# Low weight parts by accumulating DMAs in the first five pairs, no arithmetic on GpSimd in the turn, and a later T3, in a two-layer encoder kernel

## The chip, the cores and the metric

The kernel runs on one core of a Trainium2 chip. A core has five engines, each with its own in-order queue: TensorE (PE in the profile, with PEld for its weight loads), VectorE (DVE), ScalarE (ACT), GpSimd (POOL) and SyncE (SP), which here only issues DMAs. The metric is the device time of one execution in microseconds (us).

## The reference, cut to what matters

Two layers of a streaming encoder over 16 + 1024 frames of width 1024. Each layer has an attention part and then a gated feed-forward part; the change lies at the seam between the two.

```python
h = h + jnp.concatenate([o_gla, o_fox], axis=-1) @ w_out[i]
h = h + conv_ffn(rms_norm(h, ffn_norm[i]), w_up[i], conv_w[i], conv_b[i], w_down[i])

def conv_ffn(x, w_up, conv_w, conv_b, w_down):
    h = x @ w_up
    ...
    u, g = jnp.split(hc, 2, axis=-1)
    return (jax.nn.silu(g) * u) @ w_down
```

`w_up` is 1024 by 2 x 2816; between the product and the gate stands a causal depthwise convolution of width 3. Everything is float32. The kernel keeps that precision on PE by splitting each operand into a high part, rounded to the type fp32r, and a low part, the rest; one product is three matrix products (high x high, low x high, high x low).

## The kernel before

**Layout.** Activations are held transposed: 128 channels on the partitions, frames along the free axis. The frames are cut into two halves of 520 (516 in the last layer, which drops the meta frames at the end).

**Output projection** (`wout`, L1083). Eight tiles of output channels, first over one half of the frames, then over the other. After each tile DVE adds the result to the residual (L1095), POOL stores it to memory (L1096), ACT squares it and the square is added to an accumulator `acc` (L1102): on POOL, except for the last two tiles of the second half, on DVE. `scale(h)` turns `acc` of a half into the normalising factor: a matmul with ones, then DVE, ACT twice, DVE three times (L1074, L271 to L275). In the second half the operands of the first half of the frames are already made (`first_operand`, L1079) between the tiles.

**Up projection** (`ffn_up`). The 22 pairs of a `u` and a `g` tile are multiplied by a scheme of Strassen and Winograd: the blocks are (first or second half of the inner dimension) by (first or second half of the frames) and each pair takes seven products instead of eight. The products are numbered p = 1 to 7. Each has a weight operand (`up_operand`) and an activation operand `X[p]`:

| p | weight operand | activation operand | made by |
|---|---|---|---|
| 1, 2 | A11, A12 | the scaled first half | `first_operand` |
| 6 | S2 = S1 - A11 | T2 | `make_t23` |
| 7 | A11 - A21 | T3 | `make_t23` |
| 4 | A22 | N4 | `make_n4` |
| 5 | S1 = A21 + A22 | T1 | `make_t1` |
| 3 | A12 - S2 | B22 | `make_b22` |

The activation operands are made once per layer, in the turn from the output projection to the up projection. `put` makes the two parts of each: a cast on ACT (L1037), a subtraction on DVE (L1038). T2 takes a multiplication (L1132) and an addition (L1133) on DVE ahead of that for each of its four tiles; N4 a subtraction on POOL (L1144); T1 an operation on DVE (L1151) and a subtraction on POOL (L1152).

**Order.** PE's order is written out in `seq`: (0,1), (0,2), (1,1), (1,2), (2,1), (2,2), then (0,6), (1,6), (0,7), (1,7), (0,4), (1,4), (0,5), (1,5), (0,3), (1,3), then the rest of pair 2, then pair after pair, (pair, product) each. A product is 24 matmuls: four tiles of the inner dimension, two chunks of frames, three parts. `before` says ahead of which position each activation operand is written into the program: 1 `second_half` (the factor of the second half), 2 `make_t23`, 7 `make_n4`, 9 `make_t1`, 12 `make_b22`. The order on the other engines is made ahead of time by a scheduler, which takes the instruction earliest in the program among those that it takes to be ready; once made it is fixed, and each engine waits at the head of its queue.

**Banks.** Products gather in eight PSUM banks, two per accumulator. The second product of pairs 0, 1 and 2 uses the same two banks for all three pairs (`place`): (1,2) can start when (0,2) has been added out, and (2,2) when (1,2) has, by the DVE addition L1180. Products 1, 6, 7 and 4 are copied out by ACT (L1181).

**Weights.** SP loads quarter blocks of 256 KB into buffers. A11 and A12 have four buffers of their own (`raw`); A21, A22, S1, S2 and the two blocks of pair 2 that are needed early share seven (`raw2`). DVE makes the combinations (L997). `up_split` makes the parts, in six buffers each (three for even, three for odd positions): the high one with a cast on ACT (L1013), the low one with a subtraction on DVE (L1014). `ensure(i)` prepares operands up to four positions ahead of the product.

After product 3 of a pair come the convolution (ACT L1169, DVE L1173), the gate (L1198, L1202) and the store of the result by a DMA that POOL issues (L1203).

Of the kernel before, what the change touches and what calls it, by code (L numbers as in the profile page):

```python
# [10 lines left out]
F32 = mybir.dt.float32  # L11
# [3 lines left out]
ALU = mybir.AluOpType  # L15
# [33 lines left out]
HALVES, HALVES_LAST = (0, 520, 520), (8, 524, 516)  # L49
AHEAD = 4  # L50
NSPLIT = 4


class Slots:
# [78 lines left out]
class Kern:  # L133
# [731 lines left out]
    def attention(self, lyr, nm, hsrc, chunks, feed):  # L865
        tc, nc, s = self.tc, self.nc, self.slots
        with tc.tile_pool(name=f"aps{lyr}", bufs=2, space=PSUM, reuse_waits="tile") as pp2, \
# [50 lines left out]
            with tc.tile_pool(name=f"att{lyr}", bufs=2, reuse_waits="tile") as ap, \  # L918
# [5 lines left out]
                def plan(p):  # L924
# [11 lines left out]
                    elif p == 4:  # L936
# [10 lines left out]
                        def split(j):  # L947
                            c0, n = CH[j]
                            for k in KORD:
                                self.split(mix[k][0][:, c0:c0 + n], mix[k][1][:, c0:c0 + n], land[k][:, c0:c0 + n])  # L950
                            for m in range(NSPLIT):
                                nc.gpsimd.dma_start(hT[m][:, c0:c0 + n], hsrc[m][:, c0:c0 + n])
                        split(2)
                        for m in range(NSPLIT):
                            def ev(ps, c0, n, m=m):
                                h = hT[m][:, c0:c0 + n]
                                nc.vector.tensor_tensor(out=h, in0=ps, in1=h, op=ALU.add)
# [3 lines left out]
                self.fox(lyr, ap, pp, qs, plan, lambda: box["mix"][KD - 1])  # L961
            for m in range(NSPLIT, KD):
                nc.sync.dma_start(box["hT"][m][:, chunks[0][0]:T], hsrc[m][:, chunks[0][0]:T])
# [15 lines left out]
    def up_operand(self, lyr, j, p, fw, raws, odd):  # L979
        nc = self.nc  # L980
        if j == 2 and p in (1, 2):
            src = fw.tile([128, 4, 128], F32, tag="raw2", name="raw2")
            nc.sync.dma_start(src[:], self.wm[lyr, M_UP + 4][:, 4 * p - 4:4 * p, :])
            return self.up_split(src, fw, odd)
        if j not in raws:
            u, g = self.wm[lyr, M_UP + 2 * j], self.wm[lyr, M_UP + 2 * j + 1]
            q = raws[j] = {}
            for name, src, k0, own in (("A11", u, 0, True), ("A21", g, 0, False), ("A22", g, 4, False), ("A12", u, 4, True)):
                q[name] = self.wp.tile([128, 4, 128], F32, tag="raw", name="raw", bufs=4) if own else \
                    fw.tile([128, 4, 128], F32, tag="raw2", name="raw2")  # L990
                nc.sync.dma_start(q[name][:], src[:, k0:k0 + 4, :])
        q = raws[j]

        def combine(out, a, b, op):
            if out not in q:
                q[out] = fw.tile([128, 4, 128], F32, tag="raw2", name="raw2")
            nc.vector.tensor_tensor(out=q[out][:], in0=q[a][:], in1=q[b][:], op=op)  # L997
        if p == 6:
            combine("S1", "A21", "A22", ALU.add)
            combine("S2", "S1", "A11", ALU.subtract)  # L1000
        elif p == 7:
            combine("A21", "A11", "A21", ALU.subtract)
        elif p == 3:
            combine("A12", "A12", "S2", ALU.subtract)
        src = q[{1: "A11", 2: "A12", 3: "A12", 4: "A22", 5: "S1", 6: "S2", 7: "A21"}[p]]
        return self.up_split(src, fw, odd)

    def up_split(self, src, fw, odd):
        nc = self.nc
        pool, x = (fw, "2") if odd else (self.wp, "")  # L1010
        hi = pool.tile([128, 4, 128], F32R, tag="hi" + x, name="hi", bufs=3)
        lo = pool.tile([128, 4, 128], F32R, tag="lo" + x, name="lo", bufs=3)
        nc.scalar.copy(hi[:], src[:])  # L1013
        nc.vector.tensor_tensor(out=lo[:], in0=src[:], in1=hi[:].bitcast(F32), op=ALU.subtract)  # L1014
        return [(hi[:, k, :], lo[:, k, :]) for k in range(4)]

    def ffn_up(self, lyr, mix, hT, pp, fw, halves, o0, during_last):
        nc, s = self.nc, self.slots
        W = halves[2]
        n = W // 2  # L1020
        sl = [slice(c, c + W) for c in halves[:2]]
# [10 lines left out]
        def operand(x):  # L1032
            X[x] = [[s.get(F32R, f"x{x}", (128, 2, 520)) for _ in range(2)] for _ in range(2)]

        def put(x, k, src, lo=None):
            hi_, lo_ = (X[x][i][k // 2].t[:, k % 2, :W] for i in range(2))
            nc.scalar.copy(hi_, src)  # L1037
            (lo or nc.vector).tensor_tensor(out=lo_, in0=src, in1=hi_.bitcast(F32), op=ALU.subtract)  # L1038
# [17 lines left out]
        def ensure(i):  # L1056
            while len(ops) < min(i + AHEAD + 1, len(seq)):
                ops.append(self.up_operand(lyr, *seq[len(ops)], fw, raws, len(ops) % 2))


        acc, sq = s.get(F32, "r"), half_slot("sq")
# [5 lines left out]
        def scale(h):  # L1067

            ps, r = bank2("ssq", 3), acc[:, sl[h]]
            for c in range(2):  # L1070
                nc.tensor.matmul(ps[:, c, :n], self.ones[:], acc[:, halves[h] + c * n:halves[h] + c * n + n],
                                 start=True, stop=True)
            vv, y0, a = half(tmp[0], 0), half(tmp[0], 1), half(tmp[1], 0)
            nc.vector.tensor_scalar(out=two(vv), in0=used(ps), scalar1=1.0 / D, scalar2=EPS, op0=ALU.mult, op1=ALU.add)  # L1074
            self.rsqrt(r, vv, y0, a)
# [7 lines left out]
        def wout(i, h):  # L1083
            m = orders[h][i]
            k0 = KD - 1 if m < NSPLIT else 0

            def f(w):
                if h == 1 and i == KD - 1:
                    ensure(0)
                ps = bank2("wo", i % 4)  # L1090
                for k in range(len(w)):
                    for c in range(2):
                        self.mm3(ps[:, c, :n], w[k], mix[k0 + k], halves[h] + c * n, n, k == 0, k == len(w) - 1)
                x = hT[m][:, sl[h]]
                nc.vector.tensor_tensor(out=two(x), in0=used(ps), in1=two(x), op=ALU.add)  # L1095
                nc.gpsimd.dma_start(self.hm[m][:, sl[h]], x)  # L1096
                if i == 0:
                    nc.scalar.activation(acc[:, sl[h]], x, AF.Square)
                else:
                    t = half(sq, i % 2)  # L1100
                    nc.scalar.activation(t, x, AF.Square)
                    (nc.vector if h and i > 5 else nc.gpsimd).tensor_tensor(out=acc[:, sl[h]], in0=acc[:, sl[h]], in1=t, op=ALU.add)  # L1102
                if h == 0:
                    return
                if m < NSPLIT:
                    nc.scalar.mul(half(gt, m % 2), x, gain(m))
                else:
                    nc.vector.scalar_tensor_tensor(out=diff(m - 4), in0=x, scalar=gain(m), in1=half(gt, m % 2),
                                                   op0=ALU.mult, op1=ALU.subtract)
                if i == 1:  # L1110
                    scale(0)
                    operand(1)
                    operand(2)
                for k in turn.get(i, ()):
                    first_operand(k)
            return (self.wm[lyr, M_WO + m][:, k0:KD, :], f)
# [5 lines left out]
        lowk, highk, t0, t1 = hT[:4], hT[4:], sl[0], sl[1]  # L1122
# [2 lines left out]
            scale(1)  # L1125
            s.put(sq, *tmp)

        def make_t23():
            operand(6)
            for k in range(4):  # L1130
                x, y = diff(k), lowk[k][:, t0]
                nc.vector.tensor_tensor(out=x, in0=x, in1=acc[:, t1], op=ALU.mult)  # L1132
                nc.vector.tensor_tensor(out=y, in0=x, in1=y, op=ALU.add)  # L1133
                put(6, k, y)
            operand(7)
            for k in range(4):
                put(7, k, diff(k))
            s.put(*dd)

        def make_n4():  # L1140
            operand(4)
            for k in range(4):
                x = highk[k][:, t0]
                nc.gpsimd.tensor_tensor(out=x, in0=x, in1=lowk[k][:, t0], op=ALU.subtract)  # L1144
                put(4, k, x)

        def make_t1():
            operand(5)
            for k in range(4):
                x, y = highk[k][:, t1], lowk[k][:, t0]  # L1150
                nc.vector.scalar_tensor_tensor(out=x, in0=x, scalar=gain(4 + k), in1=acc[:, t1], op0=ALU.mult, op1=ALU.mult)  # L1151
                nc.gpsimd.tensor_tensor(out=y, in0=x, in1=y, op=ALU.subtract)  # L1152
                put(5, k, y)
            s.put(acc, *lowk)

        def make_b22():
            operand(3)
            for k in range(4):
                put(3, k, highk[k][:, t1])
            s.put(*highk)  # L1160
        before = {1: second_half, 2: make_t23, 7: make_n4, 9: make_t1, 12: make_b22}


        st = {}
# [45 lines left out]
        for i, (j, p) in enumerate(seq):  # L1210
# [3 lines left out]
            q = st.setdefault(j, {})  # L1214
# [219 lines left out]
```

## Time and profile before

| | |
|---|---|
| median of 3 runs | 2649.35 us (2644.81 to 2653.99) |
| profiled execution | 2645.09 us, of which the span from first to last instruction is 2643.3 |
| mean granted PE clock | 0.987 |
| busy in the span | PE 95%, PEld 91%, DVE 67%, ACT 47%, POOL 17% |
| DMA | 240.72 MB, mean 91 GB/s |
| turn of layer 0, turn of layer 1 | around 590 to 670 us, around 1898 to 1980 us |

Busy rows give the time in which an engine worked; a PE row does not tell that PE was at full clock, which the granted clock in the windows does. In rows of groups the first number behind the bar is the time in all, the second the mean in ns of one, and behind the second bar stands the idle time of the engine just before, with what ended it. In rows by source line three numbers are the shortest, the median and the longest in ns. Instructions of one engine that follow each other closely overlap a little: a DVE instruction listed with 0.69 us starts 0.61 us after the one before.

### The profile page before, as it was taken

Reading aid. Unit: us, or ns where it says so; the run is one execution under the profiler, and the core shown is the slowest. Engines: PE = TensorE matmul, PEld = TensorE weight load, DVE = VectorE, ACT = ScalarE, POOL = GpSimd, SP = SyncE. Lnnn points to the kernel's source line nnn. Section 1 sums busy time; section 2 is a strip of 40 time slices with the busy share of each in tenths; the row PEclk is TensorE's granted clock in tenths of the full one; section 3 lists DMA queues with packets and bytes.
Section 4 is the critical chain, followed back from the end, with each engine's and each line's share of the span. In section 5 each row is a group of like instructions: output and inputs, shape, how many; then the busy total and the mean of one; then the engine's idle time right before and its main releaser. Section 6 shows DMA issues by size and latency. Waiting matters only on the chain.

```text
span 2643.3 us, 46336 instructions
## 1 busy us (share of the span) xinstructions
PE 2523.9 (95%) x18102; PEld 2407.2 (91%) x18102; DVE 1759.9 (67%) x3484; ACT 1240.1 (47%) x2677; POOL 457.9 (17%) x596
## 2 busy tenths in 40 slices
PE   8999999897999999999999999998989999999997
PEld 7988898897999999999999888887889999998886
DVE  7655676759877777643665666666698767776335
ACT  6345665645544445421343565665455444453112
POOL 4033333333000000000201333332320000000002
PEclk9999999998999999999999999999999999999999
DMA  3222124341222222632312222142512222245222
GB/s 125 65 83 70 47 83 124 106 131 58 97 81 76 85 77 92 217 94 58 103 56 65 75 72 74 56 138 91 158 51 85 83 81 77 83 139 189 65 55 77
DMA packets 114476, 240.72 MB, mean 91 GB/s; under 512 B 14432, under 2 KB 36192, under 8 KB 114256
## 3 DMA queue, kind: packets, MB, share of 16 engines
q1 hardware_dynamic: 96000, 182.27, 22.7%
q0 software_dynamic: 16384, 53.18, 5.5%
q8 instruction: 142, 2.33, 0.4%
q10 hardware_dynamic: 1872, 2.31, 0.2%
q14 instruction: 78, 0.64, 0.1%
HBM read 174.01 MB, written 50.91 MB: 85 GB/s over the span
## 4 chain that ended last, share of the span: by engine, by line
PE 77%; DVE 13%; ACT 4%; issue 3%; DMA 2%; POOL 2%; DVEq 0%; SPq 0%; POOLq 0%; ACTq 0%
PE mm L216 12%; PE mm L217 12%; PE mm L218 12%; PE up L216 10%; PE up L217 10%; PE up L218 10%; PE av L706 2%; PE tr L688 2%; DVE S L655 1%; DVE x L1038 1%; PE wo L217 1%; PE wo L216 1%; PE wo L218 1%; DVE PT L331 1%; ACT P L667 1%
## 5 line engine op out<-in xcount | busy, mean ns | idle before, releaser
L216 PE MATMUL up<-x,hi 128*128 128x260 f32 (+1 forms) x2464 | 701.3, 285 | 22.7 <-DVE hu L1180 20.3
L217 PE MATMUL up<-x,lo 128*128 128x260 f32 (+1 forms) x2464 | 699.2, 284 | 0.0
L218 PE MATMUL up<-x,hi 128*128 128x260 f32 (+1 forms) x2464 | 698.5, 283 | 0.0
L216 PEld LDWEIGHTS up<-x,hi 128*128 128x128 f32 x2464 | 467.5, 190 | 24.4 <-DVE hu L1180 20.7
L217 PEld LDWEIGHTS up<-x,lo 128*128 128x128 f32 x2464 | 467.9, 190 | 0.1
L218 PEld LDWEIGHTS up<-x,hi 128*128 128x128 f32 x2464 | 467.8, 190 | 0.0
L216 PE MATMUL mm<-xh,hi 128*128 128x348 f32 (+4 forms) x1056 | 365.1, 346 | 0.0
L218 PE MATMUL mm<-xl,hi 128*128 128x348 f32 (+4 forms) x1056 | 340.9, 323 | 0.0
L217 PE MATMUL mm<-xh,lo 128*128 128x348 f32 (+4 forms) x1056 | 340.8, 323 | 0.0
L1014 DVE TENSOR_TENSOR lo<-raw,hi 128x512 fp32r<-128x512 f32 x308 | 212.9, 694 | 146.2 <-ACT hi L1013 146.2
L183 ACT CAST hi<-raw 128x512 fp32r<-128x512 f32 (+1 forms) x264 | 142.3, 543 | 329.8 <-PE mm L218 240.0
L217 PE MATMUL mm<-ah,lo 128*128 128x400 f32 (+1 forms) x760 | 266.4, 351 | 0.2 <-DVE lo L185 0.2
L218 PE MATMUL mm<-al,hi 128*128 128x400 f32 (+1 forms) x760 | 265.9, 350 | 0.0
L216 PE MATMUL mm<-ah,hi 128*128 128x400 f32 (+1 forms) x760 | 265.8, 350 | 0.0
L185 DVE TENSOR_TENSOR lo<-raw,hi 128x512 fp32r<-128x512 f32 (+1 forms) x196 | 120.7, 620 | 181.1 <-ACT hi L183 177.5
L1013 ACT CAST hi<-raw 128x512 fp32r<-128x512 f32 x308 | 190.3, 620 | 107.6 <-PE up L218 92.7
L216 PEld LDWEIGHTS mm<-xh,hi 128*128 128x128 f32 x1056 | 201.0, 190 | 6.0 <-issue 5.3
L217 PEld LDWEIGHTS mm<-xh,lo 128*128 128x128 f32 x1056 | 200.9, 190 | 0.4 <-issue 0.3
L218 PEld LDWEIGHTS mm<-xl,hi 128*128 128x128 f32 x1056 | 199.9, 189 | 0.4 <-issue 0.3
L1203 POOL DMA_DIRECT2D actd<-cv x44 | 23.4, 533 | 830.0 <-DVE cv L1202 830.0
L667 ACT ACTIVATE P<-S,m 116x460 f32<-116x460 f32 (+2 forms) x224 | 124.8, 561 | 76.9 <-DVE m L655 72.6
L331 DVE TENSOR_TENSOR PT<-tr,PT 116x464 fp32r<-116x464 f32 (+3 forms) x240 | 122.1, 516 | 55.8 <-ACT PT L330 54.1
(248 smaller groups left out, 5269.0 us busy)
## 6 DMA issues: line engine op xcount, KB each, us to landing
raw<-in_wm_dram SPq DMA_DIRECT2D x328, 256.0 KB, 2.6
raw<-in_wd_dram SPq DMA_DIRECT2D x64, 256.0 KB, 2.6
actd<-cv POOLq DMA_DIRECT2D x22, 520.0 KB, 2.9
st<-actd SPq DMA_DIRECT2D x22, 520.0 KB, 4.9
actd<-cv POOLq DMA_DIRECT2D x22, 512.0 KB, 3.0
st<-actd SPq DMA_DIRECT2D x22, 512.0 KB, 4.8
cb<-cd SPq DMA_DIRECT2D x16, 520.0 KB, 4.2
kA<-kA SPq DMA_DIRECT2D x24, 260.0 KB, 3.8
```

The lines of the kernel that those rows point to most:

```text
L183: nc.scalar.copy(hi[:, :n, :], raw[:, :n, :])
L185: eng.tensor_tensor(out=lo[:, :n, :], in0=raw[:, :n, :], in1=hi[:, :n, :].bitcast(F32), op=ALU.subtract)
L216: nc.tensor.matmul(ps, wh, xh[:, c0:c0 + n], start=first, stop=False, skip_group_check=more)
L217: nc.tensor.matmul(ps, wl, xh[:, c0:c0 + n], start=False, stop=False, skip_group_check=more)
L218: nc.tensor.matmul(ps, wh, xl[:, c0:c0 + n], start=False, stop=last, skip_group_check=more)
L331: nc.vector.tensor_tensor(out=lo, in0=src, in1=hi.bitcast(F32), op=ALU.subtract)
L655: nc.vector.tensor_tensor_reduce(out=S[:rows, :n], in0=S[:rows, :n], in1=cb[:rows, c0:k1], scale=1.0, scalar=(BIG if ci == 0 else m[:rows, ...
L667: nc.scalar.activation(P[:rows, :n], S[:rows, :n], AF.Exp, scale=-1.0, bias=m[:rows, nch - 1:nch], accum_out=(den if nch == 1 else d3[:row ...
L688: nc.tensor.transpose(tr[:w, j, :rows], P[:rows, o:o + w], id_)
L706: nc.tensor.matmul(av[:, a:width], w.rearrange("p a b -> p (a b)"), x, start=(t == 0 and i == 0), stop=(t == last and i == 1))
L1013: nc.scalar.copy(hi[:], src[:])
L1014: nc.vector.tensor_tensor(out=lo[:], in0=src[:], in1=hi[:].bitcast(F32), op=ALU.subtract)
```

## The change

Four things are altered, all in the turn and in the up projection.

1. For the first five pairs (`N_DMA_LO`), DVE does not make the low weight part. ACT writes minus the high part into the low buffer, and a DMA issued by POOL adds the raw weights to it in place.
2. For the same pairs S1 = A21 + A22 is not made by DVE: SP loads A21's block a second time into S1's buffer, and a DMA issued by POOL adds A22's block from memory.
3. POOL does no arithmetic in the turn: the sums of squares and the subtractions of N4 and T1 move to DVE.
4. `make_t23` is cut into `make_t2` and `make_t3`. T2 stays ahead of position 2, T3 goes ahead of 7, N4 from 7 to 8, T1 from 9 to 10; B22 stays.

```diff
+N_DMA_LO = 5
...
+            if j < N_DMA_LO:
+                q["S1"] = fw.tile([128, 4, 128], F32, tag="raw2", name="raw2")
+                nc.sync.dma_start(q["S1"][:], g[:, 0:4, :])
+                nc.gpsimd.dma_start(q["S1"][:], g[:, 4:8, :], accum_op=ALU.add)
...
         if p == 6:
-            combine("S1", "A21", "A22", ALU.add)
+            if "S1" not in q:
+                combine("S1", "A21", "A22", ALU.add)
             combine("S2", "S1", "A11", ALU.subtract)
...
-        return self.up_split(src, fw, odd)
+        return self.up_split(src, fw, odd, j < N_DMA_LO)
...
         nc.scalar.copy(hi[:], src[:])
-        nc.vector.tensor_tensor(out=lo[:], in0=src[:], in1=hi[:].bitcast(F32), op=ALU.subtract)
+        if by_dma:
+            nc.scalar.mul(lo[:], hi[:].bitcast(F32), -1.0)
+            nc.gpsimd.dma_start(lo[:].bitcast(F32), src[:], accum_op=ALU.add)
+        else:
+            nc.vector.tensor_tensor(out=lo[:], in0=src[:], in1=hi[:].bitcast(F32), op=ALU.subtract)
...
-                    (nc.vector if h and i > 5 else nc.gpsimd).tensor_tensor(out=acc[:, sl[h]], in0=acc[:, sl[h]], in1=t, op=ALU.add)
+                    nc.vector.tensor_tensor(out=acc[:, sl[h]], in0=acc[:, sl[h]], in1=t, op=ALU.add)
...
-        def make_t23():
+        def make_t2():
             operand(6)
...
+        def make_t3():
             operand(7)
...
-                nc.gpsimd.tensor_tensor(out=x, in0=x, in1=lowk[k][:, t0], op=ALU.subtract)
+                nc.vector.tensor_tensor(out=x, in0=x, in1=lowk[k][:, t0], op=ALU.subtract)
...
-                nc.gpsimd.tensor_tensor(out=y, in0=x, in1=y, op=ALU.subtract)
+                nc.vector.tensor_tensor(out=y, in0=x, in1=y, op=ALU.subtract)
...
-        before = {1: second_half, 2: make_t23, 7: make_n4, 9: make_t1, 12: make_b22}
+        before = {1: second_half, 2: make_t2, 7: make_t3, 8: make_n4, 10: make_t1, 12: make_b22}
```

More of the change, by code (lines that the diff above doesn't have):

```diff
@@ L983, in up_operand @@
             nc.sync.dma_start(src[:], self.wm[lyr, M_UP + 4][:, 4 * p - 4:4 * p, :])
-            return self.up_split(src, fw, odd)
+            return self.up_split(src, fw, odd, True)
         if j not in raws:
@@ L1005, in up_operand, with up_split @@
         src = q[{1: "A11", 2: "A12", 3: "A12", 4: "A22", 5: "S1", 6: "S2", 7: "A21"}[p]]
-        return self.up_split(src, fw, odd)
-    def up_split(self, src, fw, odd):
+        return self.up_split(src, fw, odd, j < N_DMA_LO)
+    def up_split(self, src, fw, odd, by_dma):
         nc = self.nc
```

## The prediction

> **What bounds the kernel now.** I read the page first (busy shares and costliest groups), then the waits of the matrix engine, then the windows around the place where the up projection begins, then single instructions there.
>
> ```profile
> PE 2523.9 (95%) x18102; PEld 2407.2 (91%) x18102; DVE 1759.9 (67%) x3484; ACT 1240.1 (47%) x2677; POOL 457.9 (17%) x596
> ...
> L216 PE MATMUL up<-x,hi 128*128 128x260 f32 (+1 forms) x2464 | 701.3, 285 | 22.7 <-DVE hu L1180 20.3
> ```
>
> TensorE (PE) is busy 95% of the span, so only its idle or slowed stretches can be won. Up projection matmuls wait 22.7 us in all, and 20.3 of that is for one kind of instruction, the VectorE (DVE) addition L1180. The waits of PE say how often:
>
> ```profile
> PE up L216 <- DVE hu L1180: 20.3, 2, 10.2
> ...
> PE up L216 <- ACT hu L1181: 2.1, 2, 1.1
> ```
>
> Two waits, one per layer, 10.2 us the longest; then one of 1.1 per layer for a ScalarE (ACT) copy. Where that is in layer 0, and what it does to the clock, is in the windows (length, busy time and count of PE, PEld, DVE, ACT, POOL, granted clock, DMA share, GB/s):
>
> ```profile
> 600.00:610.00 10.00, 6.20 (x28) 5.95 (x28) 8.93 (x14) 5.80 (x11) 3.60 (x3) 0.66 0.39 132
> ...
> 612.70:628.20 15.50, 15.49 (x125) 15.00 (x123) 14.28 (x23) 7.76 (x13) 3.44 (x3) 1.00 0.10 36
> 628.20:638.46 10.26, 0.01 (x2) 0.01 (x1) 9.04 (x12) 6.15 (x11) 4.46 (x4) 0.61 0.00 1
> 638.46:643.90 5.44, 5.44 (x25) 5.44 (x26) 4.77 (x8) 1.14 (x2) 0.00 (x0) 0.50 0.36 99
> 643.90:656.70 12.80, 11.75 (x97) 11.54 (x96) 12.64 (x14) 7.30 (x13) 6.61 (x4) 0.99 0.06 21
> ...
> 740.00:760.00 20.00, 20.00 (x170) 20.00 (x168) 14.68 (x20) 9.69 (x14) 0.53 (x1) 1.00 0.24 80
> ```
>
> A product is 24 matmuls. At full clock 170 of them take 20 us, 0.118 each, 2.8 us a product. The first five products run from 612.7 to 628.2. The sixth, (2,2), then waits 10.26 us and runs at clock 0.50: 25 matmuls in 5.44 us where 2.9 would do, 2.5 lost. Four more follow with 1.05 us idle. By 740 PE is full with DVE at 14.68 of 20: what DVE is relieved of that late is worth nothing. So the price of the turn is 10.26 + 2.5 + 1.05 = 13.8 us in layer 0; over both layers 20.3 + 2.1 + 5.0 = **27.4 us**. This is the ceiling of what the turn can return.
>
> (2,2) waits because its bank of PSUM is that of (1,2), which L1180 has not yet added out. The DVE timeline shows what that addition stood behind (start, duration, last column idle time):
>
> ```profile
> 618.45 1.29 DVE L997 TENSOR_TENSOR raw<-raw,raw 128x512 f32<-128x512 f32 x2
> ...
> 621.48 0.69 DVE L1014 TENSOR_TENSOR lo<-raw,hi 128x512 fp32r<-128x512 f32 x1
> 622.08 0.70 DVE L275 SCALAR_TENSOR_TENSOR r<-nt 128x520 f32<-128x520 f32 x1
> 622.69 0.69 DVE L997 TENSOR_TENSOR raw<-raw,raw 128x512 f32<-128x512 f32 x1
> 623.30 1.31 DVE L1132 TENSOR_TENSOR dd<-dd,r 128x520 f32<-128x520 f32 x2
> ...
> 629.42 0.70 DVE L1038 TENSOR_TENSOR x<-h,x 128x520 fp32r<-128x520 f32 x1 [2.38 <-ACT x L1037]
> ...
> 631.26 1.78 DVE L1038 TENSOR_TENSOR x<-dd,x 128x520 fp32r<-128x520 f32 x1
> ...
> 634.19 2.38 DVE L1038 TENSOR_TENSOR x<-dd,x 128x520 fp32r<-128x520 f32 x2
> ...
> 637.71 0.69 DVE L1180 TENSOR_TENSOR hu<-up,hu 128x520 f32<-128x520 f32 x1
> ```
>
> The scale r is done at 622.78. (1,2) ends at 625.3 (628.20 less one product), its addition starts at 637.71: behind T2 (12 instructions), T3's four low parts, and holes. The holes belong to GpSimd (POOL), which computes N4 at the same time:
>
> ```profile
> 625.31 4.14 POOL L1144 TENSOR_TENSOR h<-h,h 128x520 f32<-128x520 f32 x2 [11.01 <-DVE h L1133]
> ...
> 628.24 1.15 ACT L1037 CAST x<-h 128x520 fp32r<-128x520 f32 x2 [2.36 <-POOL h L1144]
> ...
> L1152 POOL TENSOR_TENSOR h<-h,h x8: 1586/1710/1771, 647.5 to 1962.9; 128x520 f32<-128x520 f32 x4, 128x516 f32<-128x516 f32 x4
> ```
>
> ACT stands 2.36 us at an N4 cast that needs POOL, T2's next cast is behind it, and DVE waits 2.38 for that. And DVE instructions of the same form that take 0.69 alone take 1.78 beside a POOL subtraction: two tensor inputs on both engines seem to exclude each other.
>
> **The change part by part.** Prices from these rows (median or mean ns, us to landing for DMAs):
>
> ```profile
> L1014 DVE TENSOR_TENSOR lo<-raw,hi 128x512 fp32r<-128x512 f32 x308 | 212.9, 694 | 146.2 <-ACT hi L1013 146.2
> L1013 ACT CAST hi<-raw 128x512 fp32r<-128x512 f32 x308 | 190.3, 620 | 107.6 <-PE up L218 92.7
> ...
> L1102 POOL TENSOR_TENSOR r<-r,sq x24: 1285/1314/2561, 559.6 to 1912.0; 128x520 f32<-128x520 f32 x12, 128x516 f32<-128x516 f32 x12
> L1102 DVE TENSOR_TENSOR r<-r,sq x4: 681/689/697, 607.0 to 1922.8; 128x520 f32<-128x520 f32 x2, 128x516 f32<-128x516 f32 x2
> ...
> L1096 POOL DMA_DIRECT2D hm<-h x32 | 17.7, 552 | 91.6 <-DVE h L1095 89.5 <-DVE lo L185 2.1
> ...
> q0 software_dynamic: 16384, 53.18, 5.5%
> ...
> raw<-in_wm_dram SPq DMA_DIRECT2D x328, 256.0 KB, 2.6
> ...
> hm<-h POOLq DMA_DIRECT2D x16, 260.0 KB, 2.6
> ...
> kA<-kA SPq DMA_DIRECT2D x24, 260.0 KB, 3.8
> ...
> L991 SPq DMA_DIRECT2D raw<-in_wm_dram x176: 327/328/433, 540.8 to 2321.7; - x176
> ...
> SPq L991 <- DVE raw L997: 39.9, 4, 18.3
> ```
>
> 1. *T2 and its addition.* DVE starts follow each other by 0.61 (622.08, 622.69, 623.30), so that is what one costs in a full queue. Ahead of r, one L1014, one S1 sum of the pair at 618.45 and another L1014 go: up to 1.8 us, of which I take 1.0, since r hangs on two ACT steps as well: r at 621.8. Then 12 x 0.61 = 7.3, one S2 combination 0.6, and L1180 itself 0.7: 630.4. PE runs dry at 628.2, so **2.2 us** of the wait remain per layer. Bounds: 0.8 (r 1.8 earlier, the addition ahead of T2's last low part) and 5.1 (r no earlier, T3's four still ahead: 622.8 + 16 x 0.61 + 0.7 = 633.3). A wait of this size leaves the clock alone: the 1.05 us idle after 643.90 left it at 0.99.
> 2. *N4 and T1 without POOL.* Eight subtractions a layer, 4 x 0.61 = 2.4 us of DVE each for N4 and T1, in place of POOL's 1.6 to 1.7 each and the DVE time it excluded. Due dates are kept: after 630.4 the work is T3 2.4, N4 4.9, T1 3 x 4 x 0.61 = 7.3, and six others 3.7, done by 649. (0,4), which needs N4, is the fifth product after (2,2) and starts at 630.4 + 5 x 2.8 = 644, N4 is done by 638; (0,5), which needs T1, starts at 650, T1 is done by 645. The 1.1 us wait for ACT, caused by its standing at T1 casts, goes.
> 3. *Sums of squares on DVE.* Twelve a layer. Seven fall in the first half of the output projection, where PE waits little for DVE; the other five, 5 x 0.61 = 3.1 us, fall in the second, where DVE is full (8.93 of 10 in the window of 600). What leaves it there, between 590 and 612:
>
> ```profile
> L1014 DVE TENSOR_TENSOR lo<-raw,hi 128x512 fp32r<-128x512 f32 x4 | 2.7, 684 | 1.4 <-ACT hi L1013 1.4
> ...
> L1102 POOL TENSOR_TENSOR r<-r,sq 128x520 f32<-128x520 f32 x3 | 6.0, 2011 | 0.3 <-ACT sq L1101 0.2
> ```
>
>    Four low parts, 2.7 us, and POOL's share of the exclusion. I take 0, bounds -2 to +2 a layer.
> 4. *Low parts by DMA.* Per operand: one DVE instruction (0.69) out; in come an ACT pass (0.62), a POOL issue (0.55) and an accumulating DMA. ACT then does 0.62 more per 2.8 us on top of 9.69 in 20: 70%, covered. POOL 0.55 in 2.8, covered. In the queue of POOL the next low parts and the stores of results stand behind a DMA that waits for its ACT pass. The trace has no accumulating DMA; nearest are the store of 260 KB (2.6 us) and the copy within SBUF (3.8). I take 3.8, from SBUF to SBUF like this one; below 2.6 I see no reason to go, above 7.6, since one more reading of the target cannot more than double it.
>    In the steady part an operand's buffer is free five products (14 us) ahead and it needs 0.62 + 0.62 + 0.55 + 7.6 = 9.4 at worst: covered. In the turn it is a chain. S1 now takes one of seven buffers for each of pairs 0 and 1 from the start, so the weights of (2,2) are loaded only when (2,1)'s low part has landed, and S2 of (0,6) finds a buffer only when that of (2,2) has. From 612.7 (the output projection's last buffer is free): 1.8 (ACT twice and the issue) + 3.8, load 2.6, 1.8 + 3.8, combination 0.7, 1.8 + 3.8 = 20.1, thus 632.8; (0,6) starts at 630.4 + 2.8 = 633.2. No slack, and S2 stands in DVE's queue among T2. I take **2.0 us** per layer, bounds 0 and 9 (at 7.6 the chain is 11 later, part of it behind the wait of point 1).
> 5. *S1 by DMA.* Five DVE additions a layer out, a load and an accumulating load in (SP's issue of 0.33 is hidden in its waits for buffers, up to 18.3). Covered, but for the chain above.
> 6. *T3 later.* It leaves the place ahead of L1180; its due date is (0,7), two products after (0,6), at 639, and DVE is at it by 631.
>
> Sum: 27.4 - 2 x 2.2 - 2 x 2.0 = 19 us. The profiled execution took 2645.09 (span 2643.3 and 1.8 around it), so 2626; the median of the runs, 2649.35, lies 4.3 above it, so **2630**. With the bounds of points 1 to 4, 27.4 - 1.6 + 4 = 30 gained at best and 27.4 - 10.2 - 18 - 4 = 5 lost at worst; I hold 10 to 29 gained, 2620 to 2640, for this case.
>
> The Trainium skill, TensorE: Matmul & The Clock Gate, Part 1 (The HAM clock gate), says that the clock falls to half after an idle window of about 3.4 us and needs as long busy to come back. The trace agrees for the long wait (clock 0.61, then 0.50 for 5.44 us). By this rule the two residual waits of a layer, if they fell together into 4.2 us, would bring the half clock back and cost 5 us over both layers: an estimate of 2635 in place of 2630.
>
> **The rivals.**
>
> *The chain of landings is the new wait.* For it: seven buffers, three landings in a row, DVE's order fixed beforehand, so a late buffer blocks T2 too. Against: S2 of pair 1 and (0,7) were prepared in time before. Each us of landing above 3.8 costs about 3 a layer; at 5.5 that is 10 in all: 2640, in a band of 2636 to 2650. Chance 0.20.
>
> *More than the turn.* In 600 to 610 PE made 28 matmuls where 10 us hold 85; 6.6 us a layer are lost to casts and low parts late in full queues. If half of it goes with POOL's exclusion: 2623; with all of it 2617. Against: DVE gets as much as it loses there. Chance 0.08.
>
> *Slower: the DMA engines become the bound.* q0 moved 53.18 MB in 5.5% of 2643.3 us, 0.72 us of all engines for 0.262 MB. In 2.8 us per product 24% is taken, S1's two transfers take 0.2 more, so 1.9 is left. Reading the target as well makes it 1.4: room. Should adding cost three passes or more (2.2 and up), the five pairs run at its pace: 70 operands, each beyond 1.9; from 2.2 the 19 us are eaten. At three and a half passes, 2.5: 70 x 0.6 - 19 = 23 slower, 2672. For it: nothing here shows an addition on the way. Chance 0.17.
>
> *It does not do what it says:* the addition of (1,2) stays behind T3 and N4 because the order of DVE is made beforehand. Then POOL's holes alone go, which leaves point 1's 5.1 a layer: 2636, within the first case's range and 0.05 of its chance.
>
> **How the numbers follow.** First case 0.55 (2620 to 2640, faster), more than the turn 0.08 (faster), chain of landings 0.20 (0.12 faster, 0.08 the same), DMA-bound 0.17 (slower). A change under 0.3%, 8 us, cannot be told from none: the three runs lie 2644.81 to 2653.99. So 0.75 faster, 0.08 same, 0.17 slower. The range runs from 2611 (27.4 and 13 of the output projection, less 2) to 2654 (worst bound of the first case), leaving out most of the DMA-bound case.
>
> **What would show it.** Right: PE's longest wait in the up projection under 5 us, for L1180 or a low part; clock 1.0 throughout 612 to 660; no POOL arithmetic between 550 and 670; low parts landing 3 to 5 us after issue. Wrong: PE waiting for a DMA of lo in many products of the first five pairs, or DVE waiting for a landing within T2, or (0,7) waiting for T3.

## The result, and the profile after

The change makes the kernel slower by 0.2%: 2653.63 us (2649.76 to 2657.95, 12 runs) against 2647.24 (2644.60 to 2653.99, 12 runs), a ratio of 1.0021, 95% interval 1.0011 to 1.0030. The forecast was 2630, faster, in a range of 2611 to 2654; the measured time lies at the slow end of that range, on the other side of no change. The profiled execution took 2652.14 us, its span 2650.4.

From the page of the changed kernel (lines have moved: L1180 is now L1194, L1181 L1195, L1014 L1026, L1013 L1021, L997 L1002, L1037 and L1038 are L1049 and L1050, L216 to L218 are L217 to L219; new are the accumulating DMAs, L1024 for low parts and L996 for S1):

```profile
PE 2533.1 (96%) x18102; PEld 2415.8 (91%) x18102; DVE 1712.7 (65%) x3444; ACT 1279.0 (48%) x2747; POOL 462.6 (17%) x636
...
q0 software_dynamic: 27904, 74.16, 10.1%
...
L217 PE MATMUL up<-x,hi 128*128 128x260 f32 (+1 forms) x2464 | 701.5, 285 | 14.4 <-DVE hg L1194 7.8
L218 PE MATMUL up<-x,lo 128*128 128x260 f32 (+1 forms) x2464 | 700.1, 284 | 4.3 <-DMA lo<-raw 4.3
...
lo<-raw POOLq DMA_DIRECT2D x70, 256.0 KB, 4.6
```

DVE is relieved of 47 us and POOL issues 80 more DMAs. The one large wait of before, 20.3 us for L1180, is gone. In its place stand three, as the waits of PE show (time in all, number, longest):

```profile
PE up L217 <- DVE hg L1194: 7.8, 3, 4.3
...
PE up L217 <- ACT x L1049: 6.5, 2, 3.6
...
PE up L218 <- DMA lo<-raw: 4.3, 2, 2.3
```

One of each per layer (the third for hg is small). Where they are, in layer 0 and then in layer 1, and the clock behind them, in the windows (columns as before):

```profile
630.00:637.20 7.20, 4.34 (x25) 4.38 (x26) 5.96 (x11) 5.71 (x12) 2.59 (x3) 0.76 0.65 126
642.60:647.10 4.50, 4.47 (x24) 4.47 (x25) 4.50 (x8) 0.83 (x2) 0.85 (x1) 0.62 1.07 225
664.20:670.40 6.20, 3.05 (x26) 2.84 (x24) 1.41 (x3) 1.33 (x3) 0.86 (x1) 0.97 1.10 225
670.40:674.80 4.40, 4.36 (x25) 4.39 (x26) 3.15 (x4) 3.72 (x5) 0.86 (x1) 0.66 0.66 179
...
1945.20:1949.60 4.40, 4.40 (x25) 4.40 (x26) 2.92 (x6) 2.69 (x6) 0.86 (x1) 0.65 0.73 126
...
1954.80:1958.20 3.40, 3.40 (x28) 3.40 (x29) 3.40 (x7) 1.50 (x4) 0.86 (x1) 1.00 1.12 178
...
1982.40:1988.50 6.10, 6.10 (x32) 6.10 (x33) 4.90 (x6) 5.27 (x6) 0.00 (x0) 0.58 0.47 137
```

All but one of the six waits, that ahead of 1954.8, are followed by a product at about half clock: 25 matmuls take 4.34 or 4.36 us and 24 take 4.47, where 0.119 each (168 matmuls in 20.00 us between 674 and 694) would make 3.0 and 2.9. That is 4.4 us lost in layer 0 and, by the same count, 3.7 in layer 1. With the 18.6 of waits it is 26.7 us, about the 27.4 that were the ceiling before: the turn was freed, and the same time was lost again. The third row also shows DVE working 1.41 us of 6.20, with the DMA engines full (1.10).

What DVE was doing there, in its timeline:

```profile
624.48 1.30 DVE L1145 TENSOR_TENSOR h<-dd,h 128x520 f32<-128x520 f32 x2
627.75 0.69 DVE L1002 TENSOR_TENSOR raw<-raw,raw 128x512 f32<-128x512 f32 x1 [1.97 <-DMA lo<-raw]
...
632.02 0.69 DVE L1194 TENSOR_TENSOR hu<-up,hu 128x520 f32<-128x520 f32 x1
...
661.52 0.70 DVE L1194 TENSOR_TENSOR hg<-up,hg 128x520 f32<-128x520 f32 x1 [0.42 <-PE up L219]
668.99 0.69 DVE L1002 TENSOR_TENSOR raw<-raw,raw 128x512 f32<-128x512 f32 x1 [6.76 <-DMA raw<-in_wm_dram]
669.60 0.69 DVE L1194 TENSOR_TENSOR hg<-up,hg 128x520 f32<-128x520 f32 x1
```

At 668.99 DVE makes S2 of pair 3. It has stood idle for 6.76 us until the accumulated S1 of that pair landed, and the addition of pair 1's hg, whose product was long done, stood behind it; product (1,3) needs that addition's bank and starts at 670.4. The order of DVE's instructions in the program is the one that the last three rows show: hg of pair 0, S2 of pair 3, hg of pair 1.

The first two rows of the timeline are another case, in the middle of T2: S2 of pair 0 waits 1.97 us for a buffer that a low part's landing frees. (2,2) starts at 632.86, right behind the hu addition that ends at 632.71. The row of waits names an ACT cast for it, the releaser that came last by the profile, but this addition is the one that PE needed.

The span is 7.1 us longer, but from the first up projection matmul to the first of the stage behind it the two layers took 456.9 and 461.1 us, against 459.2 and 459.7 before: 0.9 less together. The rest of the span, whose instructions stand in the same order in both kernels but for the sums of squares in the output projections, took 1732.4 against 1724.4. In the profiles of the other kernels below it takes anything from 1722.7 to 1732.9, so one profiled execution can't place the last 0.2%, and its cause stays open. What the runs can settle is where the 20 us went that were expected.

### The profile page after: what moved, and what is told of

The parts are those of the page before. It is cut to its first block, busy times and chain, and to the rows that moved or that the text cites. A ratio compares the mean times of both kernels' runs of the same rounds, so it can differ in the third digit from the quotient of the medians.

```text
span 2650.4 us, 46528 instructions
## 1 busy us (share of the span) xinstructions
PE 2533.1 (96%) x18102; PEld 2415.8 (91%) x18102; DVE 1712.7 (65%) x3444; ACT 1279.0 (48%) x2747; POOL 462.6 (17%) x636
## 3 DMA queue, kind: packets, MB, share of 16 engines
q0 software_dynamic: 27904, 74.16, 10.1%
## 5 line engine op out<-in xcount | busy, mean ns | idle before, releaser
L217 PE MATMUL up<-x,hi 128*128 128x260 f32 (+1 forms) x2464 | 701.5, 285 | 14.4 <-DVE hg L1194 7.8
L218 PE MATMUL up<-x,lo 128*128 128x260 f32 (+1 forms) x2464 | 700.1, 284 | 4.3 <-DMA lo<-raw 4.3
L219 PE MATMUL up<-x,hi 128*128 128x260 f32 (+1 forms) x2464 | 699.4, 284 | 0.0
L217 PEld LDWEIGHTS up<-x,hi 128*128 128x128 f32 x2464 | 468.4, 190 | 15.5 <-issue 7.8
L218 PEld LDWEIGHTS up<-x,lo 128*128 128x128 f32 x2464 | 469.1, 190 | 4.7 <-DMA lo<-raw 4.7
L219 PEld LDWEIGHTS up<-x,hi 128*128 128x128 f32 x2464 | 469.1, 190 | 0.0
L217 PE MATMUL mm<-xh,hi 128*128 128x348 f32 (+4 forms) x1056 | 366.4, 347 | 0.0
L219 PE MATMUL mm<-xl,hi 128*128 128x348 f32 (+4 forms) x1056 | 342.1, 324 | 0.0
L218 PE MATMUL mm<-xh,lo 128*128 128x348 f32 (+4 forms) x1056 | 341.9, 324 | 0.0
L218 PE MATMUL mm<-ah,lo 128*128 128x400 f32 (+1 forms) x760 | 266.4, 351 | 0.0
L219 PE MATMUL mm<-al,hi 128*128 128x400 f32 (+1 forms) x760 | 265.4, 349 | 0.0
L217 PE MATMUL mm<-ah,hi 128*128 128x400 f32 (+1 forms) x760 | 265.4, 349 | 0.0
L1026 DVE TENSOR_TENSOR lo<-raw,hi 128x512 fp32r<-128x512 f32 x238 | 162.9, 685 | 136.4 <-ACT hi L1021 136.4
L1021 ACT CAST hi<-raw 128x512 fp32r<-128x512 f32 x308 | 190.1, 620 | 101.6 <-PE up L219 84.4
L186 DVE TENSOR_TENSOR lo<-raw,hi 128x512 fp32r<-128x512 f32 (+1 forms) x196 | 110.5, 567 | 174.8 <-ACT hi L184 171.0
L217 PEld LDWEIGHTS mm<-xh,hi 128*128 128x128 f32 x1056 | 202.1, 191 | 6.0 <-issue 5.3
L218 PEld LDWEIGHTS mm<-xh,lo 128*128 128x128 f32 x1056 | 201.7, 191 | 0.4 <-issue 0.3
L219 PEld LDWEIGHTS mm<-xl,hi 128*128 128x128 f32 x1056 | 200.7, 190 | 0.4 <-issue 0.3
L218 PEld LDWEIGHTS mm<-ah,lo 128*128 128x128 f32 x760 | 142.8, 188 | 13.5 <-DVE lo L186 0.5
```

Source lines behind the costliest of these rows:

```text
L186: eng.tensor_tensor(out=lo[:, :n, :], in0=raw[:, :n, :], in1=hi[:, :n, :].bitcast(F32), op=ALU.subtract)
L217: nc.tensor.matmul(ps, wh, xh[:, c0:c0 + n], start=first, stop=False, skip_group_check=more)
L218: nc.tensor.matmul(ps, wl, xh[:, c0:c0 + n], start=False, stop=False, skip_group_check=more)
L219: nc.tensor.matmul(ps, wh, xl[:, c0:c0 + n], start=False, stop=last, skip_group_check=more)
```

## The experiments

Twelve kernels, each timed in five rounds beside the kernel before. The sum of the rows in which PE's up projection matmuls wait goes with the ratio; the change is slower than its 18.6 suggests, since nearly all its waits bring the half clock. The last column is the time of the two up projections together in the profiled execution, counted as above (918.9 before). e1 and e11, which are one kernel, give 900.5 and 901.1 there, so it is steadier than the whole.

| kernel | median us | ratio to before, interval | PE's waits in up, us | up projections, us |
|---|---|---|---|---|
| the change | 2653.63 | 1.0021 [1.0011, 1.0030] | 18.6 | 918.0 |
| e1 turn only | 2629.51 | 0.9932 [0.9916, 0.9949] | 7.9 | 900.5 |
| e2 S1 by DVE | 2636.05 | 0.9949 [0.9930, 0.9968] | 5.5 | 901.7 |
| e3 DMA parts only | 2661.23 | 1.0051 [1.0031, 1.0071] | 32.7 | 935.0 |
| e4 two pairs | 2637.51 | 0.9960 [0.9946, 0.9975] | 11.6 | 906.2 |
| e5 S1 not of pair 2 | 2643.95 | 0.9990 [0.9980, 1.0000] | 15.0 | 915.7 |
| e6 S1 from pair 2 on | 2649.43 | 1.0013 [1.0001, 1.0024] | 17.9 | 918.8 |
| e7 moves only | 2631.58 | 0.9935 [0.9919, 0.9951] | 11.7 | 905.6 |
| e8 order only | 2635.37 | 0.9953 [0.9937, 0.9968] | 12.5 | 907.6 |
| e9 S1 only | 2633.05 | 0.9936 [0.9920, 0.9953] | 6.6 | 899.6 |
| e10 T2 in halves | 2630.19 | 0.9925 [0.9910, 0.9941] | 6.2 | 900.3 |
| e11 e1 again | 2633.09 | 0.9932 [0.9913, 0.9950] | 7.9 | 901.1 |
| e12 S2 in order | 2639.69 | 0.9972 [0.9960, 0.9984] | 11.9 | 910.0 |

The kernel before had medians of 2645.68 to 2650.27 beside them, so the ratios compare better than the medians.

**The two halves of the change.** e1 keeps what is done in the turn (GpSimd's arithmetic on VectorE, T2 before T3) and makes all low parts and S1 on VectorE; e3 keeps the DMAs alone, with arithmetic and order as before.

```diff
 # e1, against the change
-N_DMA_LO = 5
+N_DMA_LO = 0
...
-            return self.up_split(src, fw, odd, True)
+            return self.up_split(src, fw, odd, False)
```

> Landing theory (the losses come from DVE instructions that stand in DVE's queue waiting for a DMA to land, and the turn part alone wins what was forecast of it): with no accumulating DMA at all the time is 0.991 to 0.994 of before (16 to 24 us faster), PE waits less than 8 us in all in the up projection, and the half clock shows at most once per layer. Turn theory (eight subtractions and twelve additions more on DVE cost as much as GpSimd's absence gives, and the DMA parts are what helps): 0.999 to 1.005, with PE waiting 15 us or more for DVE. Outside theory (the loss lies in stages that the change does not touch): the stages outside the turn are back to the times of before, whatever the turn does.

> The DMA parts of the change with GpSimd's arithmetic and the old place of T3. Landing theory: slower than the change, 1.003 to 1.010 of before: the landings block DVE as in the change, and GpSimd's subtractions now stand in one queue with the DMA issues. Turn theory: faster than the change, 0.995 to 0.999 of before.

The waits of PE, e1 and then e3:

```profile
PE up L217 <- DVE hu L1194: 4.5, 2, 3.3
PE up L217 <- DVE hg L1194: 1.6, 2, 1.2
PE up L219 <- DVE x L1050: 1.4, 2, 0.7
PE up L217 <- ACT x L1049: 0.4, 1, 0.4
```

```profile
PE up L217 <- DVE hu L1194: 17.1, 2, 8.6
PE up L217 <- DVE hg L1194: 9.9, 2, 6.4
```

e1 is 18.8 us below before, and the repeat (e11) 17.2. e3 leaves most of the old wait (17.1 of 20.3) and adds 9.9 for hg: 13 us slower. So the turn gave most of what it should, and the DMAs took it back.

> The turn part alone once more, beside the two others: 2626 to 2634, ratio 0.992 to 0.995 if its first measurement holds; over 0.997 if it was chance.

**Which DMAs.** e2 makes S1 on VectorE and leaves the low parts to the DMAs. e4 has the DMAs for two pairs in place of five. e9 has S1 by DMA and every low part on VectorE.

```diff
 # e2
-            if j < N_DMA_LO:
+            if False:
                 q["S1"] = fw.tile([128, 4, 128], F32, tag="raw2", name="raw2")
 # e4
-N_DMA_LO = 5
+N_DMA_LO = 2
 # e9
-        return self.up_split(src, fw, odd, j < N_DMA_LO)
+        return self.up_split(src, fw, odd, False)
```

> Low parts by DMA as in the change, S1 by DVE again. Landing theory: the wait of 3.2 to 4.3 us for the addition hg near 670 and 1982 and the half clock behind it go (about 6.5 us per layer), the waits in the first ten products stay: about 13 us under the change, 0.996 to 0.998 of before. Turn theory: within 3 us of the change, since DVE has five additions more per layer. If the buffers of the first pairs matter most, the first wait for (2,2) falls too and the time is below 0.995.

> Low parts and S1 by DMA for pairs 0 and 1 (and the two early blocks of pair 2) alone. Landing theory: the DMA share after 660 us falls from about 1.0 to under 0.6, pair 2's S1 is DVE's own, the wait near 670 goes; the waits in the first ten products stay: 0.996 to 0.998 of before. Turn theory: the same as the change within 3 us, or slower, as DVE takes 21 low parts per layer back.

> The turn part and S1 by DMA for all five pairs; every low part made by VectorE. Shared-engines theory (the accumulating load of S1 lands late because the accumulating low parts fill the DMA engines beside it; a DMA share of 1.1 was seen at 660 to 670): without them the share there is under 0.7, S1's load takes 3 to 4.5 us in place of 6.6 and 7.3, no wait for hg or hu over 1.5 us near 670 and 1982; 2626 to 2634, ratio 0.992 to 0.995. Issue-too-late theory (its buffer comes free too late, whatever the engines do): the wait of 3 to 5 us with its half clock stays in each layer, 2638 to 2644, ratio 0.996 to 0.999.

The longest wait of PE, a window and a row of DVE's waits, all of e2; then the longest wait of PE in e9 and two rows of DVE's timeline there:

```profile
PE up L217 <- DVE hu L1194: 5.1, 2, 3.8
```

```profile
674.00:694.00 20.00, 20.00 (x169) 20.00 (x169) 11.30 (x13) 13.76 (x22) 7.00 (x9) 1.00 1.00 241
```

```profile
DVE raw L1002 <- DMA lo<-raw: 28.7, 15, 5.3
```

```profile
PE up L217 <- DVE hu L1194: 4.9, 2, 3.4
```

```profile
662.62 0.70 DVE L1194 TENSOR_TENSOR hg<-up,hg 128x520 f32<-128x520 f32 x1
...
663.82 0.70 DVE L1194 TENSOR_TENSOR hg<-up,hg 128x520 f32<-128x520 f32 x1
```

By the ratios, low parts by DMA alone cost 0.17% over e1 (4.5 us), S1 by DMA alone 0.04% (1 us), and both together 0.89% (24 us). The first two lie within the intervals; in the up projections the three are 1 us, none and 17 us. Neither is dear; the two together are. e2 came out faster than the landing theory had it (0.996 to 0.998). The e2 window speaks against the DMA engines as the bound: their share is 1.00 for 20 us, and PE works all 20 at clock 1.00. e9 was as the theory of shared engines had it, and yet does not show it: with VectorE full of low parts, its order is another, and the two hg additions follow each other without S2 of pair 3 between them. So engines and order both fit, which e12 was then made for.

**Which pair.** The expectations of e5 and e6 take the wait near 670 for one of pair 2.

```diff
 # e5
-            if j < N_DMA_LO:
+            if j < N_DMA_LO and j != 2:
 # e6
-            if j < N_DMA_LO:
+            if 2 <= j < N_DMA_LO:
```

> The change, but S1 of pair 2 alone is made by VectorE again; the other four pairs' S1 and all low parts stay with the DMAs. Place theory (the loss of S1 by DMA is one wait a layer: VectorE meets S2 of pair 2 before S1's accumulating transfer has landed, and the evacuation of pair 2 stands behind it): the wait of PE for hg of 3 to 5 us near 670 (and 1982 in the second layer) goes with its half clock, the waits among the first ten products stay; 11 to 15 us below the change, 2639 to 2643, ratio 0.996 to 0.998. Volume theory (each S1 transfer costs the same, by the share of the DMA engines that it takes): one of five goes, 3 to 4 us below the change, 2650, ratio 1.001, and a wait of some kind stays near 670.

> The change, but S1 of pairs 0 and 1 is made by VectorE again; S1 of pairs 2, 3 and 4 and all low parts stay with the DMAs. Place theory: the wait for hg near 670 stays (3 to 5 us a layer with its half clock), since S1 of pair 2 is still loaded, and the waits for low parts and for the buffer of (2,2) among the first ten products shrink from 5 to 6 us a layer to 2 to 4: 2645 to 2650, ratio 0.999 to 1.001. Volume theory: two of five go, 7 us below the change, 2646; the wait near 670 shrinks with the share of the DMA engines, which falls from 1.1 to below 0.9 there.

Waits of PE and two windows of e5, then the longest wait of e6:

```profile
PE up L217 <- ACT x L1049: 6.8, 2, 3.4
PE up L217 <- ACT hu L1195: 6.1, 2, 4.2
PE up L218 <- DMA lo<-raw: 2.1, 2, 1.0
```

```profile
676.70:678.90 2.20, 0.28 (x4) 0.07 (x2) 2.20 (x3) 2.13 (x4) 0.25 (x1) 1.00 0.04 13
678.90:682.40 3.50, 3.50 (x16) 3.50 (x17) 3.43 (x4) 3.44 (x6) 2.20 (x4) 0.52 0.47 84
```

```profile
PE up L217 <- DVE hg L1194: 9.7, 4, 5.2
```

Neither theory came out in e5. Taking pair 2 out gave 0.3% (8 us), between the two forecasts, and a wait stayed, 8 us later and now for a copy of hu. e6 keeps the wait near 670 (5.2 us there) and gains only 0.08% (2 us) by freeing pairs 0 and 1. In all three kernels DVE resumes when the accumulating load of S1 that POOL issued for pair 3 has landed (668.99 in the change, 671.37 in e5, 668.38 in e6): the expectation had the right kind of place and the wrong pair.

**Order or engines.** e12 is the change with one thing different: S2 of pairs 2 to 4 is held behind what is written before it on VectorE. All transfers stay.

```diff
-            nc.vector.tensor_tensor(out=q[out][:], in0=q[a][:], in1=q[b][:], op=op)
+            ins = nc.vector.tensor_tensor(out=q[out][:], in0=q[a][:], in1=q[b][:], op=op)
+            if out == "S2" and 2 <= j < N_DMA_LO:
+                self.tc.keep_in_program_order(ins)
```

> The change, with S2 of pairs 2, 3 and 4 kept behind what is written before it on VectorE; nothing else differs, all transfers stay. In the change S2 of pair 3 stands between the two additions of pair 0's and pair 1's hg in VectorE's order, and VectorE stands idle 6.76 us there until the accumulated S1 of pair 3 has landed (so the wait near 670 is of pair 3, not of pair 2, as earlier expectations name it). Order theory (the loss is S2's place ahead of additions that were ready): the wait for hg of 3.5 to 4.6 us near 670 and 1982 and its half clock go, 9 to 14 us below the change, 2638 to 2645, ratio 0.996 to 0.999; the waits among the first ten products stay. Engines theory (the DMA share of 1.0 makes the transfers themselves late, whatever the order): another wait of 3 us or more, for a low part or for S2's product (3,6), comes in the next products, and the time stays within 5 us of the change, ratio 1.000 to 1.003.

Waits of PE, a window, and DVE's timeline of e12 (hg additions are at L1196 here):

```profile
PE up L217 <- ACT x L1051: 7.3, 2, 4.3
PE up L218 <- DMA lo<-raw: 2.8, 2, 1.8
PE up L217 <- DVE hg L1196: 1.3, 2, 1.2
```

```profile
660.00:675.00 15.00, 13.65 (x113) 13.27 (x112) 9.91 (x13) 10.31 (x13) 4.43 (x5) 1.00 0.96 221
```

```profile
665.22 0.69 DVE L1002 TENSOR_TENSOR raw<-raw,raw 128x512 f32<-128x512 f32 x1 [3.64 <-DMA raw<-in_wm_dram]
665.83 0.69 DVE L1196 TENSOR_TENSOR hg<-up,hg 128x520 f32<-128x520 f32 x1
...
669.07 0.69 DVE L1196 TENSOR_TENSOR hg<-up,hg 128x520 f32<-128x520 f32 x1
```

The wait for hg falls from 7.8 to 1.3 us, clock 1.00 holds through 675, and the time falls by 0.49% (13 us), with the DMA share still 0.96. Of the 13 us, 8.0 are in the up projections; the rest is little more than the two intervals leave open. For this wait it is the order that decides: one instruction with a late input, ahead of additions that were ready. A plain load of pair 3's weights still holds DVE for 3.64 us, which is left of the same kind. What remains over e1, 0.40% (11 us, 9 of them in the up projections), lies for the most part in the first ten products, where the two upper rows make 10.1 us against 4.5 in e1, with the half clock behind; e4, where the later pairs have no DMAs, has the same two waits (7.4 and 4.2 us) and lies 0.28% (7 us) over e1.

**The turn, in its two parts.** e7 moves the arithmetic and leaves T2 and T3 together; e8 does the reverse. Neither has DMAs.

```diff
 # e7, against before: the moves to VectorE, and
-        before = {1: second_half, 2: make_t23, 7: make_n4, 9: make_t1, 12: make_b22}
+        before = {1: second_half, 2: lambda: (make_t2(), make_t3()), 7: make_n4, 9: make_t1, 12: make_b22}
 # e8, against before: GpSimd keeps its arithmetic, and
-        before = {1: second_half, 2: make_t23, 7: make_n4, 9: make_t1, 12: make_b22}
+        before = {1: second_half, 2: make_t2, 7: make_t3, 8: make_n4, 10: make_t1, 12: make_b22}
```

> No accumulating DMAs; GpSimd's arithmetic moved to VectorE; T2 and T3 made together at the old places. Theory of the prediction's points 1 and 2 (the exclusion and GpSimd's casts are worth the larger part, the order of T3 the rest): the wait of (2,2) falls from 10.2 to 4 to 6 us a layer, still with its half clock, 8 to 14 us below the kernel before: 2634 to 2640, ratio 0.995 to 0.997. Rival (the order is what counts, the engine does not): within 4 us of before, ratio 0.999 to 1.001.

> No accumulating DMAs; GpSimd keeps its arithmetic; T2 at the old place, T3, N4 and T1 later as in the change. Theory of points 1 and 2: T2 no longer runs beside N4 on GpSimd, so holes and exclusion shift behind it, and (2,2) waits 3 to 6 us in place of 10.2; a second wait comes two or three products later for N4 or T3 casts: 6 to 14 us below before, 2634 to 2642, ratio 0.995 to 0.998. Rival (the engine is what counts, the order does not): (2,2) waits 8 us or more, within 4 us of before, ratio 0.999 to 1.001.

The waits of PE, e7 and then e8:

```profile
PE up L217 <- DVE hu L1194: 11.3, 2, 5.7
```

```profile
PE up L217 <- DVE hu L1194: 7.5, 2, 3.8
PE up L217 <- DVE hg L1194: 2.5, 2, 1.2
```

Either alone wins most of it (17 and 12 us by the ratios), and the two don't add: both act on what stands ahead of the same addition. e7 went further than its forecast although its waits are as forecast, 4 to 6 us a layer; by the waits it should lie 3 to 4 us above e1, which the intervals don't exclude and the up projections show (905.6 against 900.5).

**A better version?** e10 is e1 with the second half of T2 written behind the addition of (1,2).

```diff
-        before = {1: second_half, 2: make_t2, 7: make_t3, 8: make_n4, 10: make_t1, 12: make_b22}
+        before = {1: second_half, 2: lambda: make_t2((0, 1)), 4: lambda: make_t2((2, 3)), 7: make_t3, 8: make_n4, 10: make_t1, 12: make_b22}
```

> A version meant to be better than the turn part alone: no DMAs for low parts or S1, and T2 made in two halves, the second behind the addition of (1,2). If (2,2) waits for that addition behind T2 alone, as the prediction's point 1 has it, its wait falls from 3.3 and 1.2 us to under 0.5, the half clock at 631 goes, and (0,6) waits at most 1.2 us for the last of T2: 3 to 7 us below the turn part alone, 2623 to 2628, ratio 0.990 to 0.992. Rival (the order in which VectorE is given its work moves the addition no further ahead, or T2 becomes late by as much): same as the turn part alone, 2629 to 2632, ratio 0.993 to 0.994.

Its waits of PE:

```profile
PE up L219 <- DVE x L1050: 2.8, 5, 0.7
PE up L217 <- DVE hg L1195: 1.8, 2, 1.2
...
PE up L217 <- DVE hu L1195: 0.2, 1, 0.2
```

The wait for hu is gone, but others grew in its place, and the gain over e11 beside it, 2.9 us, lies within the intervals. e1, e9, e10 and e11 are one time as far as these runs tell, 0.64 to 0.75% faster than before: the change is best without its low parts by DMA, and S1 by DMA adds nothing. A larger pool of buffers in place of the seven, which might shorten the chain, wasn't tried.

## Why the prediction was wrong

**Point 5 is the step that failed.** It put S1 by DMA at nothing, "Covered, but for the chain above", since SP has time to issue the loads. It looked at the issuing queue and not at who reads the result: S2 stands in DVE's fixed order, and an input that lands late makes DVE wait with ready work behind it. That costs 13 us by the ratios (e12), 8.0 in the up projections. Leaving out S1's DMAs wins 19 (e2, 0.72%), 16 in the up projections, but part of that is point 4's: the waits in the first ten products fall from 10.8 to 5.1 us as well, where S1 no longer takes a buffer of the chain from the start (that this is why is argued, not shown). The rival about landings said that "DVE's order fixed beforehand" lets a late buffer block T2, and gave it a chance of 0.20; the same sentence, applied to every DVE instruction that reads a landing, would have led to pair 3.

Two more terms were mis-sized, and in the up projections of the profiles the account closes. Points 1, 2, 3 and 6 gained 18 us (e1 and e11) where 23 were forecast. Of these 9 are lost in e12, for the most part to the chain of point 4, where 4 were forecast. Another 8 are lost in the change, by point 5, where nothing was. That leaves 1 us in place of 19.

**Point 4** named the chain of landings rightly and sized it too small. The sign that the prediction gave for being wrong, "DVE waiting for a landing within T2", is in the timeline above: 1.97 us ahead of 627.75. The landing was taken as 3.8 us and the issue as 0.55. The answers for the source lines of the accumulating DMAs, low parts and then S1 (from DMA to landing: shortest, median, longest; for S1 also who waited for it, and how long):

```profile
DMA to landing us min/median/max: 3.2/4.6/7.6
```

```profile
  DVE raw L1002: 20.0, 3
...
DMA to landing us min/median/max: 3.9/4.4/7.5
```

Its cost in the first ten products was forecast as 2.0 us a layer. e4 and e12 lie 7 and 11 us over e1, so it is some 4 to 5 a layer at most, with the half clocks. The longest landing is the 7.6 us that the prediction took as its bound; that it meets it to the tenth is luck. That "in the steady part" the low parts are "covered" holds for PE: in e2 DVE waits 28.7 us for landings over both layers, most of it behind the turn, and can afford it, and PE waits for no low part.

**The rival of the DMA engines** fell. From the rows of q0, before and after, 10.1% of 2650.4 less 5.5% of 2643.3 is 122 us for 80 transfers: 1.5 us of all engines for each, near the 1.4 taken and below the 2.2 from which it would decide.

**Points 1, 2, 3 and 6** were right in kind and 4 to 6 us too large together. They say 27.4 - 4.4 = 23 without the DMAs; e1 and e11 measured 17 to 19. Point 1's residue was forecast as 4.4 us over both layers and is 4.5, but as 3.3 and 1.2 and not as 2.2 twice, so the match is partly luck. Its steps, in DVE's timeline of e1:

```profile
622.03 0.70 DVE L276 SCALAR_TENSOR_TENSOR r<-nt 128x520 f32<-128x520 f32 x1
...
629.95 0.70 DVE L1145 TENSOR_TENSOR h<-dd,h 128x520 f32<-128x520 f32 x1
...
631.16 0.70 DVE L1194 TENSOR_TENSOR hu<-up,hu 128x520 f32<-128x520 f32 x1
```

The factor is ready at 622.7 in place of 621.8, so the addition comes at 631.2 to 631.9 in place of 630.4. What was missed is that "a wait of this size leaves the clock alone" (below), and 3.4 us for hg and for casts, taken as nothing: 27.4 less the 7.9 of waits and the 1.6 lost at half clock is 17.9. Point 3 was put at 0, and the output projection took 61.9 and 61.4 us before, 61.9 and 62.0 after.

## What to carry to other kernels

Work moved from an engine to a DMA frees the engine's time, but gives its reader a new and longer latency: 0.7 us of DVE became landings of 3.2 to 7.6 us here. Look for that reader's place in its own in-order queue, and count what stands behind it that is ready, in every stage and not only in the one under study. If the order is made by a scheduler that counts on an earlier landing (inferred here; the runs show only that the place decided), hold the reader back behind the ready work: here that was worth 13 us by the ratios (8 in the up projections), though not as much as leaving the transfers away.

## What the runs showed of the hardware

**An accumulating DMA** of 256 KB took POOL 0.86 us to issue (the store of 260 KB 0.55) and landed in 3.2 us at the shortest and 4.6 in the median. The Trainium skill, DMA: Bandwidth & Descriptors, Anatomy of one DMA — SWDGE (gpsimd) path, gives 2.0 us plus the bytes at 436 GB/s for a transfer that GpSimd issues; by it an estimate of 2.6 us. The plain stores of 260 KB before agree with that (2.6 in the median); no accumulating transfer here reached it.

**The clock** fell to half after shorter waits than forecast, and not always. In the change a wait of 2.3 us ahead of 642.6 was enough (clock 0.62 behind it), in e5 one of 1.9 us ahead of 678.9 (0.52), while the 2.0 us ahead of 1954.8 and e12's 1.2 ahead of 666.6 left it at 1.00. The window of e1 behind its wait of 3.3 us:

```profile
631.90:636.10 4.20, 4.18 (x22) 4.19 (x23) 3.59 (x6) 0.07 (x1) 0.00 (x0) 0.59 0.38 120
```

22 matmuls in 4.18 us, where 2.6 would do. The Trainium skill, TensorE: Matmul & The Clock Gate, Part 1 (The HAM clock gate), has the clock at half after an idle window of about 3.4 us, and the window runs freely, whatever the kernel does. That two waits of about 2 us end differently agrees with a free-running window. That 1.9 us of waiting is enough does not agree with a whole window of idleness, nor with the prediction's reading, a wait of at least that length; the measurement decides, and what share of a window must be idle stays open.
